# Where weight and activation tiles start in SBUF, and when the first row scales are made: a change to a split-precision decoder trunk

## The chip, the cores and the metric

The kernel runs on one core of a Trainium2 chip. The metric is the device time of one execution, in microseconds (us); three runs before the change took 1011.95, 1014.01 and 1015.58 us, median 1014.01. The engines are TensorE (PE, its weight loads shown apart as PEld), VectorE (DVE), ScalarE (ACT), GpSimd (POOL) and SyncE (SP). [...]

## The reference

A decoder trunk of two layers over 256 tokens of width 1024, all in float32. A layer is a feed-forward block, a token mixer, and a second feed-forward block; the mixer of layer 0 is native sparse attention (nsa), that of layer 1 sliding-window attention (swa). A last norm follows.

```python
def rmsnorm(x, g):
    y = x * rsqrt(mean(x * x, axis=-1, keepdims=True) + 1e-6)
    return y * g

def swiglu(x, w_gu, w_down):             # w_gu: 1024 x 5632, w_down: 2816 x 1024
    g, u = split(x @ w_gu, 2, axis=-1)
    return (silu(g) * u) @ w_down

for i in range(2):
    x = x + 0.5 * swiglu(rmsnorm(x, ffn1_norm[i]), ffn1_w_gu[i], ffn1_w_down[i])
    x = x + mixer[i](rmsnorm(x, mix_norm[i]))
    x = x + 0.5 * swiglu(rmsnorm(x, ffn2_norm[i]), ffn2_w_gu[i], ffn2_w_down[i])
return rmsnorm(x, final_norm)
```

The program calls the four feed-forward blocks ffn0 (layer 0), ffn1 (layer 0, after the nsa mixer), ffn2 and ffn3 (layer 1, around the swa mixer).

## The kernel before, in words

**Split products.** Every float32 product is made of passes in the fp32r type. Weights are fetched as they are (`raw`, five buffers, SP's queue, line 166) and split by `Weights.split` into a high part (a cast to fp32r: tile `whi`, line 150 or 152) and a low part (raw minus high: tile `wlo`, line 178). Each of these tiles is 128 partitions by 1024 + 64 elements, and `place` says at which byte of it the part starts. Activations are transposed on PE (line 199) and split in the same way when they leave PSUM: `xh`, high and low side by side, scaled by the norm's weights out of `prm` (lines 207 and 210).

**Up and gate product** (`gu`, `product` in `ffn`). The columns of `w_gu` are taken in 22 blocks; block f gives 128 columns of the gate (bank 0) and 128 of the up half (bank 1). For each of 8 slices k of the depth and each bank there is a pair of matmuls: the high weights stay in the array while `xh` streams through, high and low together (512 columns, `gu_h`); then the low weights meet the high half of `xh` (256 columns, `gu_l`). So a block is 16 pairs, an ffn 352 pairs or 704 matmuls. Names: `gu_2_0_328` is block 2, bank 0; the last number only tells tiles apart. In ffn0 to ffn3 the high weights start at byte `PLACE_GU` = 64, 128, 192 and 32 of their tile; the low weights and `xh` start at 0. (All tiles begin at a multiple of 256 bytes.)

**Other products** (`RowsProduct`): here the activations stay in the array and the weights stream: 512 columns at a time in the down products (`dn`) and output projections, 256 in the input projections of the mixers (`nin`, `sin`) and in the last two of the three column blocks of ffn3's down product (`LASTW`). For 256 columns both weight parts start at byte 64 (`PLACE_NARROW`), for 512 at 0; the activations start at 0.

**Gate arithmetic.** After a block's last matmul ACT copies the second half of a bank out (`g`, `u`, line 150) and DVE adds the first half (lines 426 and 428). POOL multiplies both by the row scales `rb` (line 155, `ga` and `u`); ACT takes the tanh (`th`, line 430); DVE forms the gate and the product (lines 432 and 155); the result is split into `hh` and `hl` for the down product. `g`, `u`, `ga` and `th` have two buffers each, and even blocks use one pair of PSUM banks, odd blocks another, so block 4 needs the banks of block 2 emptied, and block 2's `u` needs block 0's buffer back.

**Row scales.** A norm's 1/rms per token comes from squares (DVE line 226 and ACT line 230 at the start of ffn0), `n_v` (lines 232, 234), a power on POOL (`n_y`, line 241) and a Newton step on DVE (`n_w`, `n_r`, lines 242 to 245). Two PE transposes (line 406) spread `n_r` over the partitions, and DVE copies the result to `rb` (line 407).

**Order.** The start of ffn0 (`Norm.first`) is written out by hand: its instructions go to the engines as they stand. Elsewhere a scheduler orders them by priorities; all engines then run their queues in that order. In `Norm.first` the loads of x, the identity `ident` (line 294) and the norm weights `prm` (line 296) are spread over the queues of SP and ACT.

Of the kernel before, what the change touches and what calls it, by code (L numbers as in the profile page):

```python
# [21 lines left out]
P = 128  # L22
# [23 lines left out]
PLACE_GU = (64, 128, 192, 32)  # L46
PLACE_NARROW = 64
# [41 lines left out]
def trunk_kernel(tc, x_in, wgu, wdn, nsa_in, nsa_w1, nsa_out, swa_in, swa_out, small, fgain, consts, out):  # L89
# [3 lines left out]
    with ExitStack() as es:  # L93
# [63 lines left out]
        class Weights:  # L157
# [6 lines left out]
            def fetch(self, o, w):  # L164
                raw = wp.tile([P, PIECE], F32, tag="raw", bufs=BUFS["raw"], name=f"{self.name}_r{o}")
                self.last = nc.sync.dma_start(raw[:, :w], self.src[:, o:o + w]).ins
                return raw
# [23 lines left out]


        def transposed(kp, norm, th, tl, tb, engine=None):

            ps = s_bank(f"xt{norm}_{kp}")
            for kk in range(2):
                for t in range(NT):
                    c = ((2 * kp + kk) % 4) * P
                    nc.tensor.transpose(ps[:, kk * S + t * P:kk * S + (t + 1) * P], x[t][kp // 2][:, c:c + P], ident)  # L199
            both = ap_.tile([P, 2, 2, S], F32R, tag="ahl", bufs=BUFS["ahl"], name=f"xh{norm}_{kp}")  # L200
            hi, lo = both[:, :, 0, :], both[:, :, 1, :]

            def evict(kk):
                k = 2 * kp + kk
                g = prm[:, D_GAIN + norm * KD + k:D_GAIN + norm * KD + k + 1]
                if (engine or pick("xh")) == "A":
                    nc.scalar.activation(hi[:, kk, :], ps[:, kk * S:(kk + 1) * S], AF.Copy, scale=g)  # L207
                else:
                    nc.vector.tensor_scalar(hi[:, kk, :], ps[:, kk * S:(kk + 1) * S], g, None, ALU.mult)
                nc.vector.scalar_tensor_tensor(lo[:, kk, :], ps[:, kk * S:(kk + 1) * S], g, hi[:, kk, :],  # L210
                                               ALU.mult, ALU.subtract)
# [7 lines left out]
        def squares(j, c0, c1, v, dve=False):  # L219

            ss = sp.tile([P, NT], F32, tag="ss", bufs=3, name="ss")
            for t in range(NT):
                xc = columns(t, c0, c1)
                if dve and t:
                    junk = ap_.tile([P, 512], F32, tag="junk2", bufs=1, name="junk2")
                    nc.vector.tensor_tensor_reduce(out=junk[:, :c1 - c0], in0=xc, in1=xc, scale=1.0, scalar=0.0,
                                                   op0=ALU.mult, op1=ALU.add, accum_out=ss[:, t:t + 1])
                else:
                    junk = ap_.tile([P, 512], F32, tag="junk", bufs=1, name="junk")
                    nc.scalar.activation(junk[:, :c1 - c0], xc, AF.Square, accum_out=ss[:, t:t + 1])  # L230
            if j == 0:
                nc.vector.tensor_scalar(v, ss, 1.0 / D, EPS, ALU.mult, ALU.add)
            else:
                nc.vector.scalar_tensor_tensor(v, ss, 1.0 / D, v, ALU.mult, ALU.add)

        def row_scale(v, name):
# [6 lines left out]
            nc.vector.tensor_mul(w, w, v)  # L243
            nc.vector.tensor_scalar(w, w, -0.5, 1.5, ALU.mult, ALU.add)
            nc.vector.tensor_mul(r, w, y)
            return r

        class Norm:
# [6 lines left out]
            def block(self, j):  # L255
# [7 lines left out]
                squares(j, c0, c0 + self.widths[j], self.v)  # L263
# [3 lines left out]
            def first(self, wts, product):  # L267


                def load_x(h, queues):  # L270
                    for t, queue in enumerate(queues):
                        queue.dma_start(x[t][h], x_in[t * P:(t + 1) * P, h * 512:(h + 1) * 512])
# [11 lines left out]
                zeros = ap_.tile([P, 512], BF16, tag="junk2", bufs=1, name="zeros")  # L284
# [11 lines left out]
                nc.scalar.dma_start(prm[:, :D_SINK], small[:, :D_SINK])  # L296
# [8 lines left out]
                product(0)  # L305
                wts.split(256, raw[1], 768, "AV")
                leave(1, 3)
                product(2)
                turn(2, 3)
                product(1, 3)  # L310
# [4 lines left out]
                product(4, 6, 5, 7)  # L315
                wts.load(CHUNK, CHUNK, engines="VG")
                for h in range(2):
                    squares(h, h * 512, h * 512 + 512, self.v, True)
                self.r = row_scale(self.v, "n0")


        class RowsProduct:
            def __init__(self, wts, nk, hi, lo, widths, name, tags=("acc",)):
                self.wts, self.nk, self.hi, self.lo = wts, nk, hi, lo
# [38 lines left out]
        def rows_product(wts, nk, hi, lo, done, name):  # L363
            rows = RowsProduct(wts, nk, hi, lo, done.widths, name, ("acc", "out"))
# [18 lines left out]
        def ffn(i, norm, nxt, residual=Residual):  # L383
            with tc.tile_pool(name=f"ffn{i}", bufs=1) as fp:
                wts = Weights(wgu[i], f"gu{i}", (PLACE_GU[i], 0))
# [12 lines left out]

                if i == 0:
                    acc = banks(0)  # L400
                    with tc.manual_schedule():
                        norm.first(wts, lambda *ks: product(0, acc, ks))
                rb = fp.tile([P, S], F32, name="rb")
                ps = t_bank(f"rb{i}")
                for t in range(NT):
                    nc.tensor.transpose(ps[:, t * P:(t + 1) * P], norm.r[:, t:t + 1].to_broadcast([P, P]), ident)
                nc.vector.tensor_copy(rb, ps[:, :S])
                hh, hl = [], []
                for f in range(NF):
                    if i or f:  # L410
                        if i or f > 1:
                            wts.load(f * CHUNK, CHUNK)
                        acc = banks(f)
                        product(f, acc, range(KD))
                    if i == 0 and f == 3:
                        with tc.issue_after(wts.last):
                            nc.sync.dma_start(cst[:, P:], consts[:, P:])
                            nc.sync.dma_start(prm[:, D_SINK:], small[:, D_SINK:])
                    g0 = fp.tile([P, S], F32, tag="g0", bufs=BUFS["g0"], name=f"g0{f}")
                    u0 = fp.tile([P, S], F32, tag="u0", bufs=BUFS["u0"], name=f"u0{f}")  # L420
# [4 lines left out]
                    copy("g0", g0, acc[0][:, S:])  # L425
                    nc.vector.tensor_tensor(g0, acc[0][:, :S], g0, ALU.add)  # L426
                    copy("u1", u0, acc[1][:, S:])
                    nc.vector.tensor_tensor(u0, acc[1][:, :S], u0, ALU.add)  # L428
# [9 lines left out]
                rows_product(Weights(wdn[i], f"dn{i}"), NF, hh, hl, residual(0.25, nxt), f"dn{i}")  # L438
# [120 lines left out]
        def out_tiles(name):  # L559
            both = [ap_.tile([P, 2, 2, S], F32R, tag="ahl", bufs=BUFS["ahl"], name=f"{name}_oh{g}") for g in range(NG)]  # L560
# [456 lines left out]
```

## Time and profile before

| | before |
|---|---|
| runs | 1011.95, 1014.01, 1015.58 us, median 1014.01 |
| profiled execution | 1014.02 us, of which the span of its instructions is 1011.9 us |
| busy time of PE, DVE, ACT, POOL | 977.4 (97%), 694.8 (69%), 555.8 (55%), 499.8 us (49%) |
| granted TensorE clock, mean | 0.991 |
| HBM read | 167.02 MB, 166 GB/s over the span |

A row of a timeline gives the start, the duration of one instruction (or of a run of them, with their count), the engine, the line, the operation with output and input, their shapes, and in brackets the idle time of the engine before it and what ended that. A row of windows gives from:to, the window's length, the busy time and count of each engine asked for, the granted clock (1.00 is full), the share of time in which the DMA engines were busy, and GB/s. A DMA row gives the transfer, the queue it was issued from, its count, its size and the median time from issue to landing.

### The profile page before, as it was taken

What the parts mean: (1) busy time and instruction counts of PE and PEld (TensorE: products, weight loads), DVE (VectorE), ACT (ScalarE), POOL (GpSimd) and SP (SyncE); (2) the same over time, 40 slices, a digit from 0 to 9 for tenths busy, and PEclk for the clock granted to TensorE, in tenths of its full rate; (3) what the DMA queues carried; (4) which work ended last, traced back from release to release, by engine and by line L of the source; (5) the groups of instructions that cost most, each with busy time, mean ns of one, the idle gap of its engine ahead of it and who ended that gap; (6) DMA issues with size and microseconds to landing.
All of it is one profiled execution on the core that took longest, in us unless ns stands there. A gap on an engine that the chain in (4) does not pass through costs nothing. (4 is left out here: it accounts for less than half of the span.)

```text
span 1011.9 us, 15910 instructions
## 1 busy us (share of the span) xinstructions
PE 977.4 (97%) x5626; PEld 845.2 (84%) x5626; DVE 694.8 (69%) x1299; ACT 555.8 (55%) x1041; POOL 499.8 (49%) x490
## 2 busy tenths in 40 slices
PE   7999999998899999999999999999998899999997
PEld 5888888887887788888888888888897688888897
DVE  5877754367798887778445777854279987777533
ACT  5555554456668755555444565554458755555442
POOL 2666673566354126455631566674662016554643
PEclk9999999999899999999999999999999999999999
DMA  7666656552422256666566566656652266666661
GB/s 253 207 192 189 204 173 205 172 167 84 126 84 80 67 152 198 175 202 178 183 186 205 168 205 193 191 176 213 187 150 81 71 200 188 188 187 188 187 188 42
DMA packets 47743, 169.10 MB, mean 167 GB/s; under 512 B 5424, under 2 KB 5808, under 8 KB 47664
## 3 DMA queue, kind: packets, MB, share of 16 engines
q1 hardware_dynamic: 46656, 166.43, 54.7%
q10 hardware_dynamic: 1008, 1.66, 0.4%
q8 instruction: 44, 0.72, 0.3%
q14 instruction: 35, 0.29, 0.1%
HBM read 167.02 MB, written 1.05 MB: 166 GB/s over the span
## 5 line engine op out<-in xcount | busy, mean ns | idle before, releaser
L116 PE MATMUL gu<-xh,gu_h 128*128 128x512 f32 x1408 | 490.0, 394 | 2.6 <-ACT xh L207 2.6
L116 PE MATMUL gu<-xh,gu_l 128*128 128x256 f32 x1408 | 392.3, 280 | 0.0
L116 PEld LDWEIGHTS gu<-xh,gu_h 128*128 128x128 f32 x1408 | 264.9, 189 | 61.0 <-ACT gu_h L150 3.0
L116 PEld LDWEIGHTS gu<-xh,gu_l 128*128 128x128 f32 x1408 | 265.9, 189 | 1.4 <-DVE gu_l L178 0.2
L178 DVE TENSOR_TENSOR gu_l<-gu_r,gu_h 128x1024 fp32r<-128x1024 f32 (+1 forms) x175 | 231.2, 1321 | 30.9 <-ACT gu_h L150 30.0
L150 ACT CAST gu_h<-gu_r 128x1024 fp32r<-128x1024 f32 (+1 forms) x177 | 183.7, 1040 | 42.3 <-PE gu L116 27.2
L150 ACT CAST dn_h<-dn_r 128x1024 fp32r<-128x1024 f32 (+1 forms) x89 | 92.3, 1042 | 103.4 <-PE dn L116 99.8
L116 PE MATMUL dn<-dn_h,hh 128*128 128x512 f32 (+1 forms) x396 | 144.7, 365 | 0.0
L116 PE MATMUL dn<-dn_l,hh 128*128 128x512 f32 (+1 forms) x396 | 144.7, 365 | 0.0
L116 PE MATMUL dn<-dn_h,hl 128*128 128x512 f32 (+1 forms) x396 | 144.5, 365 | 0.0
L178 DVE TENSOR_TENSOR dn_l<-dn_r,dn_h 128x1024 fp32r<-128x1024 f32 (+1 forms) x56 | 73.0, 1308 | 95.9 <-ACT dn_h L150 95.9
L178 POOL TENSOR_TENSOR dn_l<-dn_r,dn_h 128x512 fp32r<-128x512 f32 x66 | 88.7, 1365 | 99.0 <-ACT dn_h L150 98.4
L155 POOL TENSOR_TENSOR ga<-g,rb 128x256 f32<-128x256 f32 x88 | 104.0, 1182 | 62.8 <-DVE g L426 58.4
L155 POOL TENSOR_TENSOR hl<-u,hh 128x256 fp32r<-128x256 f32 x66 | 80.8, 1224 | 51.0 <-ACT hh L150 26.4
L155 POOL TENSOR_TENSOR u<-u,rb 128x256 f32<-128x256 f32 x88 | 68.6, 780 | 59.4 <-DVE u L428 57.5
L430 ACT ACTIVATE th<-ga 128x256 f32<-128x256 f32 x88 | 36.8, 419 | 100.6 <-POOL ga L155 99.5
L116 PEld LDWEIGHTS dn<-dn_h,hh 128*128 128x128 f32 x396 | 74.3, 188 | 12.0
L116 PEld LDWEIGHTS dn<-dn_h,hl 128*128 128x128 f32 x396 | 74.4, 188 | 11.8
L116 PEld LDWEIGHTS dn<-dn_l,hh 128*128 128x128 f32 x396 | 74.3, 188 | 11.8
L150 ACT COPY g<-gu 128x256 f32<-128x256 f32 x88 | 32.8, 373 | 83.4 <-PE gu L116 83.2
L432 DVE SCALAR_TENSOR_TENSOR ga<-th,ga 128x256 f32<-128x256 f32 x88 | 43.4, 493 | 37.9 <-ACT th L430 37.9
L116 PE MATMUL nin<-nin_h,xh 128*128 128x256 f32 (+1 forms) x320 | 62.8, 289 | 2.0 <-DVE r_b L459 1.7
(244 smaller groups left out, 1407.2 us busy)
## 6 DMA issues: line engine op xcount, KB each, us to landing
gu_r<-in_wgu_dram SPq DMA_DIRECT2D x174, 512.0 KB, 4.3
dn_r<-in_wdn_dram SPq DMA_DIRECT2D x87, 512.0 KB, 3.8
nin_r<-in_nsa_in_dram SPq DMA_DIRECT2D x18, 512.0 KB, 3.5
sin_r<-in_swa_in_dram SPq DMA_DIRECT2D x10, 512.0 KB, 3.5
nout_r<-in_nsa_out_dram SPq DMA_DIRECT2D x8, 512.0 KB, 3.6
sout_r<-in_swa_out_dram SPq DMA_DIRECT2D x8, 512.0 KB, 3.7
cmp_r<-in_nsa_w_dram SPq DMA_DIRECT2D x4, 512.0 KB, 4.0
nin_r<-in_nsa_in_dram SPq DMA_DIRECT2D x2, 456.0 KB, 4.0
```

Source lines behind the costliest of these rows:

```text
L116: nc.tensor.matmul(o, w, m, start=start, stop=stop)
L150: nc.scalar.copy(o, i)
L155: (nc.vector if pick(key) == "V" else nc.gpsimd).tensor_tensor(o, a, b, op)
L178: eng.tensor_tensor(lo[:, q:e], raw[:, q:e], hi[:, q:e], ALU.subtract)
L430: nc.scalar.activation(th, ga, AF.Tanh, scale=0.5)
L432: nc.vector.scalar_tensor_tensor(ga, th, 1.0, ga, ALU.add, ALU.mult)
```

## The change

1. The high parts of all four up-and-gate products start at byte 192.
2. In the narrow products the weights start at byte 0 and the activations at 64: `PLACE_NORM` for the two mixers' norms, and in ffn3 a fill of 64 bytes ahead of its tiles (`PLACE_H`), which shifts `hh` and `hl`. ffn3's one 512-wide block has its weights at 64 too. Tiles of activations get 64 elements more (`split_tile`).
3. At the start, `ident` goes to SP's queue, `prm` is second on ACT's queue, and the first 256 columns of weights come third on ACT's queue; their high part is cast on POOL instead of ACT. The squares of x's left half are taken on DVE ahead of the first evictions, those of the right half, both on DVE, after the low part of block 1.
4. The transposes of the row scales stand in block 2 of ffn0, behind its first eight matmuls, and the gate arithmetic of blocks 0 and 1 behind block 2's matmuls. The Newton step is three DVE instructions in place of four, in every norm.

The diff, cut:

```diff
-PLACE_GU = (64, 128, 192, 32)
-PLACE_NARROW = 64
+PLACE_GU = 192
+PLACE_NORM = (0, 64, 0, 0, 64, 0)
+PLACE_H = (0, 0, 0, 64)
...
+        def split_tile(name, place=0):
+            t = ap_.tile([P, 4 * S + 64], F32R, tag="ahl", bufs=BUFS["ahl"], name=name)
+            return t[:, place // 4:place // 4 + 4 * S].rearrange("p (k a t) -> p k a t", k=2, a=2)
...
-            both = ap_.tile([P, 2, 2, S], F32R, tag="ahl", bufs=BUFS["ahl"], name=f"xh{norm}_{kp}")
+            both = split_tile(f"xh{norm}_{kp}", PLACE_NORM[norm])
...
             nc.vector.tensor_mul(w, y, y)
-            nc.vector.tensor_mul(w, w, v)
-            nc.vector.tensor_scalar(w, w, -0.5, 1.5, ALU.mult, ALU.add)
-            nc.vector.tensor_mul(r, w, y)
+            nc.vector.scalar_tensor_tensor(w, w, -0.5, v, ALU.mult, ALU.mult)
+            nc.vector.scalar_tensor_tensor(r, w, 1.5, y, ALU.add, ALU.mult)
...
-                load_x(0, (nc.sync, nc.scalar))
-                nc.scalar.dma_start(ident, consts[:, C_ID:C_ID + P])
-                raw = [wts.fetch(o, n) for o, n in ((0, 256), (256, 768))]
+                load_x(0, 0, nc.sync)
+                load_x(1, 0, nc.scalar)
+                nc.sync.dma_start(ident, consts[:, C_ID:C_ID + P])
                 nc.scalar.dma_start(prm[:, :D_SINK], small[:, :D_SINK])
-                load_x(1, (nc.sync, nc.scalar))
+                raw = [wts.fetch(0, 256, nc.scalar), wts.fetch(256, 768)]
+                load_x(1, 1, nc.scalar)
+                load_x(0, 1, nc.sync)
...
+                left = squares(0, 512, "V")
                 turn(0, 1)
...
-                wts.split(0, raw[0], 256, "AG")
+                wts.split(0, raw[0], 256, "GG")
...
                 wts.load(CHUNK, CHUNK, engines="VG")
-                for h in range(2):
-                    squares(h, h * 512, h * 512 + 512, self.v, True)
+                right = squares(512, 1024, "V")
+                mean(0, self.v, left)
+                mean(1, self.v, right)
                 self.r = row_scale(self.v, "n0")
+                product(1, *range(KD))
...
-                self.wts.place = (0, 0) if w == 512 else (PLACE_NARROW, PLACE_NARROW)
+                self.wts.place = (self.place * (w == 512),) * 2
...
+                if PLACE_H[i]:
+                    fill(fp, "place", PLACE_H[i])
+                wts = Weights(wgu[i], f"gu{i}", (PLACE_GU, 0))
...
+                        if f == len(early):
+                            product(f, acc, ks[:len(early)])
+                            broadcast_scale()
+                            ks = ks[len(early):]
+                        product(f, acc, ks)
...
+                    if f == len(early):
+                        for args in left:
+                            gated(*args)
...
+                    if f < len(early):
+                        left.append((f, g0, u0))
+                    else:
+                        gated(f, g0, u0)
```

(`early` holds blocks 0 and 1 in ffn0 and is empty in the other three, where the broadcast stays ahead of block 0.)

What this does to the order at three places. On ACT, the DMAs at the program's start, before the change:

```order
L272 DMA x_73<-in_x_dram 128x512
L294 DMA ident<-in_consts_dram 128x128
L296 DMA prm<-in_small_dram 128x48
L272 DMA x_74<-in_x_dram 128x512
L299 ACT_TABLE_LOAD
L299 ACTIVATE warm<-mhalf 128x2
L207 ACTIVATE xh_0_123<-xt_0_118,prm 128x256
```

The same rows of ACT's queue after the change (`gu_r_109` are the 256 columns):

```order
L280 DMA x_73<-in_x_dram 128x512
L304 DMA prm<-in_small_dram 128x48
L168 DMA gu_r_109<-in_wgu_dram 128x256
L280 DMA x_74<-in_x_dram 128x512
L309 ACT_TABLE_LOAD
L309 ACTIVATE warm<-mhalf 128x2
L214 ACTIVATE xh_0_130<-xt_0_125,prm 128x256
```

`prm` moves ahead to second, `ident` leaves for SP's queue (second there, in the place of the 256 columns), and those 256 columns of weights come third here.

On PE, around the transposes of the row scales, before the change (the last two pairs of block 1 and the first pair of block 2):

```order
L116 MATMUL gu_1_0_265<-xh_3_168,gu_h_217 128x512
L116 MATMUL gu_1_0_265<-xh_3_168,gu_l_218 128x256
L406 MATMUL rb_244<-ident,n_r 128x128 x2
L116 MATMUL gu_1_1_266<-xh_3_168,gu_h_217 128x512
L116 MATMUL gu_1_1_266<-xh_3_168,gu_l_218 128x256
L116 MATMUL gu_2_0_328<-xh_0_123,gu_h_318 128x512
L116 MATMUL gu_2_0_328<-xh_0_123,gu_l_319 128x256
```

On PE around the same transposes after the change (block 2, slices 1 and 2 of the depth):

```order
L118 MATMUL gu_2_1_302<-xh_0_130,gu_h_291 128x512
L118 MATMUL gu_2_1_302<-xh_0_130,gu_l_292 128x256
L424 MATMUL rb_311<-ident,n_r 128x128 x2
L118 MATMUL gu_2_0_301<-xh_1_136,gu_h_291 128x512
L118 MATMUL gu_2_0_301<-xh_1_136,gu_l_292 128x256
L118 MATMUL gu_2_1_302<-xh_1_136,gu_h_291 128x512
L118 MATMUL gu_2_1_302<-xh_1_136,gu_l_292 128x256
```

The transposes move from ahead of block 1's last pair to behind block 2's fourth pair, ten matmuls later.

On DVE, from the first Newton step to the copy of `rb` and what follows it, before the change:

```order
L242 TENSOR_TENSOR n_w<-n_y 128x2
L243 TENSOR_TENSOR n_w<-n_w,n_v 128x2
L178 TENSOR_TENSOR gu_l_319<-gu_r_316,gu_h_318 128x1024
L244 TENSOR_SCALAR n_w<-n_w 128x2
L178 TENSOR_TENSOR gu_l_325<-gu_r_322,gu_h_324 128x1024
L245 TENSOR_TENSOR n_r<-n_w,n_y 128x2
L178 TENSOR_TENSOR gu_l_382<-gu_r_379,gu_h_381 128x1024
L407 COPY rb<-rb_244 128x256
L426 TENSOR_TENSOR g_299<-gu_1_0_265,g_299 128x256
L178 TENSOR_TENSOR gu_l_388<-gu_r_385,gu_h_387 128x1024
L432 SCALAR_TENSOR_TENSOR ga_250<-th_251,ga_250 128x256
```

The same stretch of DVE's queue after the change:

```order
L252 TENSOR_TENSOR n_w<-n_y 128x2
L180 TENSOR_TENSOR gu_l_292<-gu_r_289,gu_h_291 128x1024
L253 SCALAR_TENSOR_TENSOR n_w<-n_w,n_v 128x2
L180 TENSOR_TENSOR gu_l_298<-gu_r_295,gu_h_297 128x1024
L254 SCALAR_TENSOR_TENSOR n_r<-n_w,n_y 128x2
L180 TENSOR_TENSOR gu_l_381<-gu_r_378,gu_h_380 128x1024
L468 TENSOR_TENSOR g_283<-gu_1_0_90,g_283 128x256
L180 TENSOR_TENSOR gu_l_387<-gu_r_384,gu_h_386 128x1024
L470 TENSOR_TENSOR u_284<-gu_1_1_91,u_284 128x256
L425 COPY rb<-rb_311 128x256
L180 TENSOR_TENSOR gu_l_446<-gu_r_443,gu_h_445 128x1024
L439 SCALAR_TENSOR_TENSOR ga_339<-th_340,ga_339 128x256
```

The copy of `rb` had one low part between it and `n_r`; now it has two, and the additions of block 1 (`g_283`, `u_284`), with one more low part right behind it, ahead of the first gate (`ga`, line 432 before, 439 after). The addition into `u_362`, which empties block 2's second bank, follows behind a further low part.

More of the change, by code (lines that the diff above doesn't have):

```diff
@@ L217, in columns, with squares @@
             return x[t][c0 // 512][:, c0 % 512:c0 % 512 + c1 - c0]
-        def squares(j, c0, c1, v, dve=False):
+        def squares(c0, c1, engine="A"):
             ss = sp.tile([P, NT], F32, tag="ss", bufs=3, name="ss")
@@ L223, in squares @@
                 xc = columns(t, c0, c1)
-                if dve and t:
-                    junk = ap_.tile([P, 512], F32, tag="junk2", bufs=1, name="junk2")
+                junk = ap_.tile([P, 512], F32, tag="junk", bufs=1, name="junk")
+                if engine == "V":
                     nc.vector.tensor_tensor_reduce(out=junk[:, :c1 - c0], in0=xc, in1=xc, scale=1.0, scalar=0.0,
@@ L228, in squares, with mean @@
                 else:
-                    junk = ap_.tile([P, 512], F32, tag="junk", bufs=1, name="junk")
                     nc.scalar.activation(junk[:, :c1 - c0], xc, AF.Square, accum_out=ss[:, t:t + 1])
+            return ss
+        def mean(j, v, ss):
             if j == 0:
@@ L262, in block @@
                         evict(1)
-                squares(j, c0, c0 + self.widths[j], self.v)
+                mean(j, self.v, squares(c0, c0 + self.widths[j]))
                 if j == len(self.widths) - 1:
@@ L267, in first, with load_x @@
             def first(self, wts, product):
-                def load_x(h, queues):
-                    for t, queue in enumerate(queues):
-                        queue.dma_start(x[t][h], x_in[t * P:(t + 1) * P, h * 512:(h + 1) * 512])
+                def load_x(t, h, queue):
+                    queue.dma_start(x[t][h], x_in[t * P:(t + 1) * P, h * 512:(h + 1) * 512])
                 evict = {}
@@ L282, in leave @@
                         evict[k // 2](k % 2)
-                zeros = ap_.tile([P, 512], BF16, tag="junk2", bufs=1, name="zeros")
+                zeros = ap_.tile([P, 512], BF16, name="zeros")
                 nc.vector.memset(zeros, 0.0)
@@ L361, in block, with rows_product @@
                 return acc
-        def rows_product(wts, nk, hi, lo, done, name):
-            rows = RowsProduct(wts, nk, hi, lo, done.widths, name, ("acc", "out"))
+        def rows_product(wts, nk, hi, lo, done, name, place=0):
+            rows = RowsProduct(wts, nk, hi, lo, done.widths, name, ("acc", "out"), place)
             for j in range(len(done.widths)):
@@ L397, in product, with broadcast_scale, gated @@
                             do(*args)
+                early = []
                 if i == 0:
-                    acc = banks(0)
+                    early = [banks(f) for f in range(2)]
                     with tc.manual_schedule():
-                        norm.first(wts, lambda *ks: product(0, acc, ks))
+                        norm.first(wts, lambda f, *ks: product(f, early[f], ks))
                 rb = fp.tile([P, S], F32, name="rb")
[L404 to L407, printed above, removed]
-                hh, hl = [], []
[L409 to L420, printed above, removed]
+                def broadcast_scale():
+                    ps = t_bank(f"rb{i}")
+                    for t in range(NT):
+                        nc.tensor.transpose(ps[:, t * P:(t + 1) * P], norm.r[:, t:t + 1].to_broadcast([P, P]), ident)
+                    nc.vector.tensor_copy(rb, ps[:, :S])
+                hh, hl = [], []
+                left = []
+                def gated(f, g0, u0):
                     ga = fp.tile([P, S], F32, tag="ga", bufs=BUFS["ga"], name=f"ga{f}")
@@ L559, in out_tiles @@
         def out_tiles(name):
-            both = [ap_.tile([P, 2, 2, S], F32R, tag="ahl", bufs=BUFS["ahl"], name=f"{name}_oh{g}") for g in range(NG)]
+            both = [split_tile(f"{name}_oh{g}") for g in range(NG)]
             return [b[:, :, 0, :] for b in both], [b[:, :, 1, :] for b in both]
```

40 lines of the change are left out of this document (26 added, 14 removed).

## The prediction

> **What bounds the kernel now.** First the page's busy shares and slices, to see which engine the span belongs to.
>
> ```profile
> span 1011.9 us, 15910 instructions
> ...
> PE 977.4 (97%) x5626; PEld 845.2 (84%) x5626; DVE 694.8 (69%) x1299; ACT 555.8 (55%) x1041; POOL 499.8 (49%) x490
> ...
> PE   7999999998899999999999999999998899999997
> ...
> PEclk9999999999899999999999999999999999999999
> ```
>
> TensorE (PE) is busy 97% of the span, at full clock but for a start. An edit pays if PE's matmuls follow each other faster or if PE waits less; work of the other engines counts where PE ends up waiting for it. So the second view is the windows, 80 us out of the middle of each ffn's up-and-gate stage, in program order (high parts at 64, 128, 192 and 32 bytes). The columns after the window are its length and then busy time (with count) of PE, PEld, DVE, ACT and POOL, then the granted clock, the DMA share and GB/s.
>
> ```profile
> 40.00:120.00 80.00, 80.00 (x472) 70.92 (x471) 62.28 (x97) 45.17 (x78) 50.49 (x48) 1.00 0.66 192
> 385.00:465.00 80.00, 80.00 (x457) 69.85 (x456) 61.92 (x94) 45.16 (x76) 44.27 (x47) 1.00 0.64 191
> 575.00:655.00 80.00, 80.00 (x472) 70.74 (x471) 62.26 (x97) 44.77 (x77) 50.53 (x49) 1.00 0.66 195
> 845.00:925.00 80.00, 80.00 (x457) 69.77 (x457) 60.42 (x95) 44.97 (x75) 46.79 (x48) 1.00 0.65 191
> ```
>
> PE never idles in any of them and the clock is 1.00, yet ffn1 and ffn3 (128 and 32 bytes) get 457 matmuls through where ffn0 and ffn2 (64 and 192) get 472. A pair of matmuls (512 columns, then 256) takes 80/236 = 0.339 us in the one and 80/228.5 = 0.350 in the other. Those two stages are what a change of place can win. The third view is the same windows cut to the whole stages of ffn1, ffn2 and ffn3, counting the instructions of the tile `gu` alone (PE, PEld, DVE, ACT).
>
> ```profile
> 364.40:489.60 125.20, 124.67 (x704) 107.95 (x703) 17.53 (x42) 15.86 (x43) 1.00 0.63 185
> 550.40:671.50 121.10, 120.56 (x704) 105.65 (x703) 17.52 (x42) 15.65 (x42) 1.00 0.64 188
> 818.70:943.60 124.90, 124.37 (x704) 107.55 (x703) 17.52 (x42) 15.91 (x43) 1.00 0.63 186
> ```
>
> The same 704 matmuls take 124.67 and 124.37 us at 128 and 32 bytes, 120.56 at 192.
>
> **The sum, part by part.** It is made against the profiled execution, 1014.02 us (span 1011.9 and 2.1 around it), which is also the median of the runs (1014.01). 0.3% of it, 3.0 us, is about what a measurement of this kernel can tell from no change.
>
> *High parts at 192.* The arithmetic of the stages is unchanged; ffn1 and ffn3 get ffn2's place and, I take it, its pace: (124.67 − 120.56) + (124.37 − 120.56) = 7.9 us less, all on PE and so on the path. ffn0 goes from 64 to 192, and both places show 472: 0. Bounds: −7.9, and for no effect at all 0.
>
> *Narrow products.* Input projections and the last half of ffn3's down product stream 256 columns of weights, at 64 bytes, against activations at 0. Afterwards the weights lie at 0 and the activations at 64. Two pieces of the nsa input projection, and the end of ffn3:
>
> ```profile
> 284.08 0.40 PE L116 MATMUL nin<-nin_h,xh 128*128 128x256 f32 x2
> ...
> 288.32 0.40 PE L116 MATMUL nin<-nin_h,xh 128*128 128x256 f32 x2
> ```
> ```profile
> 302.01 0.39 PE L116 MATMUL nin<-nin_h,xh 128*128 128x256 f32 x2
> ...
> 305.41 0.39 PE L116 MATMUL nin<-nin_h,xh 128*128 128x256 f32 x2
> ```
> ```profile
> 980.00:1000.00 20.00, 20.00 (x172) 1.00 0.21 66
> ```
>
> 36 matmuls lie between the first two rows, 0.118 us each; 30 between the next two, 0.113 each: the same form at the same addresses runs at two paces. ffn3's end (about 170 starts in 20 us) keeps the slow one, 0.118. On the path stand 2 × 132 such matmuls in ffn3's down product and 240 in the swa input projection. Best end: all get the fast pace, 504 × 0.0047 = −2.4. Other end: the new offset costs what the bad places cost a pair, (0.350 − 0.339)/2 per matmul, 504 × 0.0055 = +2.8. The nearest row is ffn0's window: there too the stationary tile (the weights) starts 64 bytes past the moving one, and the pace is the fast one. Its stream is 512 columns wide, not 256, so I take half of the best end: −1.2. The nsa projection gets 0, since part of it is fast already.
>
> *The start.*
>
> ```profile
> ident<-in_consts_dram ACTq DMA_DIRECT2D x1, 64.0 KB, 4.0
> prm<-in_small_dram ACTq DMA_DIRECT2D x1, 24.0 KB, 7.2
> ```
> ```profile
> 1.66 0.45 ACTq L296 DMA_DIRECT2D prm<-in_small_dram  x1
> ...
> 8.93 0.47 ACT L207 ACTIVATE xh<-xt,prm 128x256 fp32r<-128x256 f32 x1 [4.81 <-DMA prm<-in_small_dram]
> 9.31 0.39 ACT L150 CAST gu_h<-gu_r 128x256 fp32r<-128x256 f32 x1
> 9.44 0.48 DVE L210 SCALAR_TENSOR_TENSOR xh<-xt,prm,xh 128x256 fp32r<-128x256 f32 x1 [8.31 <-ACT xh L207]
> ...
> 10.07 1.19 PE L116 MATMUL gu<-xh,gu_h 128*128 128x512 f32 x2 [2.56 <-ACT xh L207]
> ```
>
> The first matmul waits for an eviction, and that for the norm weights `prm`, third on ACT's DMA queue, which land 7.2 us after their issue. As second they are issued 0.48 us earlier (an issue takes 0.45). The first weights' 128 KB take their old slot as third, and if they land as late as `prm` did (8.9), the cast, now on POOL, and the first matmul come at about 9.5. `ident` on SP's queue replaces that 128 KB piece as second, so SP's later transfers issue no later. The two squares put ahead of DVE's evictions are covered by its 8.31 us of idling; ACT loses two squares and a cast. PE runs these first matmuls at half clock (windows of 3.4 us: busy time, clock):
>
> ```profile
> 9.80:13.20 3.40, 3.13 (x11) 0.50 0.24 54
> ```
>
> If full clock comes no earlier than about 13.2, starting 0.5 us earlier is worth half. I take −0.3 (0 to −0.5).
>
> *Blocks 1 to 4 of ffn0.* First, what the row scales cost now: two more of these windows, then the timelines of PE, DVE, POOL and ACT.
>
> ```profile
> 23.40:26.80 3.40, 0.99 (x7) 1.00 0.59 171
> 26.80:30.20 3.40, 3.40 (x12) 0.51 0.93 314
> ```
> ```profile
> 25.99 0.43 PE L406 MATMUL rb<-ident,n_r 128*128 128x128 f32 x2 [2.41 <-DVE n_r L245]
> ...
> 27.05 0.63 PE L116 MATMUL gu<-xh,gu_h 128*128 128x512 f32 x1
> ...
> 30.25 0.40 PE L116 MATMUL gu<-xh,gu_h 128*128 128x512 f32 x1
> ```
> ```profile
> 18.34 1.80 DVE L226 CUSTOM_DVE_ANT_0 junk<-x 128x512 f32<-128x512 f32 x1
> ...
> 21.25 0.68 DVE L226 CUSTOM_DVE_ANT_0 junk<-x 128x512 f32<-128x512 f32 x1
> ...
> 23.43 1.23 DVE L178 TENSOR_TENSOR gu_l<-gu_r,gu_h 128x1024 fp32r<-128x1024 f32 x1
> ...
> 25.78 0.15 DVE L245 TENSOR_TENSOR n_r<-n_w,n_y 128x2 f32<-128x2 f32 x1
> ...
> 26.98 0.42 DVE L407 COPY rb<-rb 128x256 f32<-128x256 f32 x1
> ...
> 36.58 0.41 DVE L428 TENSOR_TENSOR u<-gu,u 128x256 f32<-128x256 f32 x1
> ```
> ```profile
> 18.18 3.12 POOL L178 TENSOR_TENSOR gu_l<-gu_r,gu_h 128x512 fp32r<-128x512 f32 x2 [4.57 <-PE gu L116]
> ```
> ```profile
> 38.96 0.37 ACT L150 COPY g<-gu 128x256 f32<-128x256 f32 x1 [0.32 <-PE gu L116]
> ```
>
> PE waits 2.41 us for `n_r`, and the idle window is followed by one at half clock: five pairs at 0.64 instead of 0.34, 1.5 us. Together 3.9. Afterwards PE runs into block 2, whose first low part (the 23.43 row) ends at about 24.6; PE, which stopped at 23.58 with a pair of block 1 left, would want it at about 24.1 or, after the earlier start, 23.8: 0.5 to 0.8 us of waiting. Eight matmuls later (1.4 us) `n_r`, behind one more low part, is just there: 0.1 to 0.2. Too little idling for the clock. The fused row scales save a 0.16 us DVE instruction in each norm: hidden behind the low parts, 0. Gain so far 3.0.
>
> But the copy of `rb` now stands behind two low parts (1.23 each) and two additions (0.41) that were partly behind it: it ends about 2 us later on the old clock, near 29.3 for 27.4. Behind it wait POOL's multiplications of blocks 0 and 1, the tanh, DVE's two products, POOL's subtraction that frees block 0's `u` buffer, ACT's copy into that buffer, and DVE's addition, which empties block 2's second bank for block 4. In the trace the addition (36.58 row) ended 9.6 us after `rb`; block 3's first bank was done at 38.9 (last row), so there were 2 us in hand. Now it ends at 38.2 to 38.9 while PE, 3.0 earlier, wants the bank at about 36.4: a new wait of some 2.1 us. That wait is this part's dearest guess: the order shows what queues, not how long it takes. Taken: −3.0 + 2.1 = −0.9, from −3.1 (no new wait) to +1.5 (a longer one, with a window at half clock after it).
>
> [...]
>
> Sum: 1014.0 − 7.9 − 1.2 − 0.3 − 0.9 = **1003.7 us**.
>
> **Rivals.**
>
> *No new wait at block 4.* If POOL's and DVE's work behind `rb` packs better than before (ACT has less to do at the start), the 2.1 us do not appear: 1001.6. For it: 9.6 us for a chain of eight steps hold much queueing that may close up. Against: the four low parts that block 2 and 3 need are issued ahead. 25%.
>
> *The new offset is no better for narrow streams.* 0 to +2.8 in place of −1.2: 1004.9 to 1007.7. For it: the pace changes at fixed addresses, so something besides the address sets it. 20%.
>
> *Place does not matter.* ffn1 and ffn3 would be slower for another reason in their surroundings, and 7.9 + 1.2 us stay: 1012.8, within 0.3%. Against: the four windows have the same load on all engines (DMA 0.64 to 0.66, clock 1.00). 6%. [...]
>
> *Slower: the fast pace is a state that a stage falls into, not its address.* The nsa projection shows two paces at one address. If at 192, with the new start, all four stages settle in the 0.350 pace, ffn0 and ffn2 lose what ffn1 and ffn3 keep: 2 × 352 × 0.011 = +7.9, with the start and blocks −1.2: 1020.7 (narrow at 0). It decides from a mean pair of 0.349 on: 1408 × (0.349 − 0.3445) = 6.3 over the mean of now is more than 3.0 + 1.2. Against: ffn2 holds its pace at 192 for 120 us through 0.5 us of stalls (121.10 − 120.56). 4%.
>
> **How the numbers follow.** Forecast 45%, no new wait 25%, narrow no better 20%, place without effect 6%, all slow 4%. The first three are faster by over 0.3% (below 1011.0): 0.90; same 0.06; slower 0.04. The range: the low end is the rival without a new wait, 1001.6, less half a narrow gain and some of the scatter of the runs (1011.95 to 1015.58): 1000.0. The high end is narrow at its worst, 1007.7, with a little for a longer wait at block 4: 1008.5. Left out is about 15%.
>
> **What would show it.** The windows of ffn1 and ffn3 should count 472 in 80 us, their stages last 121; ffn3's end should count about 177 in 20 us for the full narrow gain. PE's wait at `rb` should be below 0.3 us and no half-clock window follow it; a wait of about 2 us should stand at block 4's second bank, with `u` as its releaser; the first `gu` matmul should start near 9.5. The forecast is wrong if a stage at 192 counts 457, or if PE's lost time between 23 and 45 us exceeds 4 us.

## The result: 1001.93 us, ratio 0.989

Four runs of the changed kernel took 1000.10, 1001.73, 1002.14 and 1006.02 us, median 1001.93; the kernel before took 1011.57 to 1015.58, median 1012.98. The ratio is 0.9894 (95% interval 0.9856 to 0.9931): 10.7 us less, between 7 and 14.6. Forecast were 1003.7 us and a range of 1000.0 to 1008.5.

The page of the changed kernel, its lines for the span and the busy shares:

```profile
span 999.9 us, 15905 instructions
...
PE 966.6 (97%) x5626; PEld 836.7 (84%) x5626; DVE 688.5 (69%) x1297; ACT 551.4 (55%) x1036; POOL 511.1 (51%) x491
```

PE is as full as before over a span 12.0 us shorter. The windows out of the middle of the four gate-and-up stages, in program order (columns as in the prediction):

```profile
40.00:120.00 80.00, 80.00 (x459) 70.13 (x458) 62.47 (x97) 44.48 (x78) 51.66 (x49) 1.00 0.67 198
385.00:465.00 80.00, 80.00 (x472) 71.00 (x472) 61.84 (x97) 45.23 (x77) 54.11 (x50) 1.00 0.66 198
575.00:655.00 80.00, 80.00 (x472) 70.76 (x471) 63.02 (x96) 46.04 (x79) 52.44 (x50) 1.00 0.67 198
835.00:915.00 80.00, 80.00 (x472) 70.76 (x471) 62.62 (x98) 44.41 (x76) 53.00 (x49) 1.00 0.66 195
```

ffn1 and ffn3 went from 457 matmuls to 472. But ffn0, which had 472 at byte 64, has 459 at 192: nearly what the bad places had. The whole stages of ffn1, ffn2 and ffn3, instructions of `gu` alone:

```profile
360.80:482.00 121.20, 120.63 (x704) 106.03 (x703) 17.52 (x42) 15.66 (x42) 1.00 0.63 187
542.60:663.80 121.20, 120.62 (x704) 105.72 (x704) 17.52 (x42) 15.65 (x42) 1.00 0.63 188
810.40:931.70 121.30, 120.65 (x704) 105.71 (x704) 17.50 (x42) 16.02 (x43) 1.00 0.65 191
```

124.67 and 124.37 us of PE became 120.63 and 120.65. The start and the row scales, as DMA rows and PE rows of ffn0:

```profile
gu_r<-in_wgu_dram ACTq DMA_DIRECT2D x1, 128.0 KB, 6.5
...
prm<-in_small_dram ACTq DMA_DIRECT2D x1, 24.0 KB, 3.8
```
```profile
8.66 0.74 PE L118 MATMUL gu<-xh,gu_h 128*128 128x512 f32 x2 [1.61 <-POOL gu_h L154]
...
22.25 0.38 PE L118 MATMUL gu<-xh,gu_l 128*128 128x256 f32 x1 [0.28 <-DVE gu_l L180]
...
23.53 0.43 PE L424 MATMUL rb<-ident,n_r 128*128 128x128 f32 x2
...
35.44 0.49 PE L118 MATMUL gu<-xh,gu_h 128*128 128x512 f32 x1 [1.32 <-DVE u L470]
```

`prm` lands 3.8 us after its issue instead of 7.2, and the first matmul, at 8.66 for 10.07, now waits for the cast of the first weights (POOL, `gu_h`), which are third on ACT's queue. The transposes at 23.53 wait for nothing. The new stop at block 4 is there, 1.32 us, with `u` as its releaser. Behind that stand, on ACT and then on DVE:

```profile
34.55 0.37 ACT L152 COPY u<-gu 128x256 f32<-128x256 f32 x1 [0.27 <-POOL hl L157]
```
```profile
34.96 0.42 DVE L470 TENSOR_TENSOR u<-gu,u 128x256 f32<-128x256 f32 x1 [1.72 <-ACT u L152]
```

POOL's subtraction frees the buffer, ACT copies into it, DVE adds: the chain of the prediction.

Where the 12.0 us of the two profiled spans came from, by first and last matmul of each stage:

| stage | before, us | after, us | difference |
|---|---|---|---|
| first `gu` matmul of ffn0 | 10.07 | 8.66 | −1.4 |
| gate and up, ffn0 | 127.12 | 127.49 | +0.4 |
| nsa input projection, with the mixer's work among it | 119.74 | 117.20 | −2.5 |
| gate and up, ffn1 | 125.31 | 121.16 | −4.2 |
| swa input projection, likewise | 40.54 | 39.95 | −0.6 |
| gate and up, ffn3 | 124.98 | 121.18 | −3.8 |
| down product, ffn3 | 61.19 | 61.19 | 0 |

The 2.5 us of the nsa mixer are in no sum of the prediction. The clock shows them. Windows of 3.4 us there (PE's busy time and count, clock), before:

```profile
242.00:245.40 3.40, 3.40 (x18) 0.52 0.52 154
252.20:255.60 3.40, 3.40 (x16) 0.51 0.38 98
265.80:269.20 3.40, 3.27 (x16) 0.50 0.44 130
```

and after, at the same distances:

```profile
241.30:244.70 3.40, 3.40 (x18) 0.51 0.53 154
251.50:254.90 3.40, 3.40 (x29) 1.00 0.46 143
265.10:268.50 3.40, 3.40 (x32) 1.00 0.53 154
```

Three stretches at half clock became one. That need not be the change's doing: another execution of the changed kernel had two (below).

### The profile page after: what moved, and what is told of

Same layout as the page of the kernel before. It is cut to its first block, busy times and chain, and to the rows that moved or that the text cites. A ratio compares the mean times of both kernels' runs of the same rounds, so it can differ in the third digit from the quotient of the medians.

```text
span 999.9 us, 15905 instructions
## 1 busy us (share of the span) xinstructions
PE 966.6 (97%) x5626; PEld 836.7 (84%) x5626; DVE 688.5 (69%) x1297; ACT 551.4 (55%) x1036; POOL 511.1 (51%) x491
## 5 line engine op out<-in xcount | busy, mean ns | idle before, releaser
L118 PE MATMUL gu<-xh,gu_h 128*128 128x512 f32 x1408 | 483.0, 391 | 2.9 <-POOL gu_h L154 1.6
L180 DVE TENSOR_TENSOR gu_l<-gu_r,gu_h 128x1024 fp32r<-128x1024 f32 (+1 forms) x175 | 228.3, 1304 | 24.3 <-ACT gu_h L152 24.1
L157 POOL TENSOR_TENSOR ga<-g,rb 128x256 f32<-128x256 f32 x88 | 113.3, 1287 | 64.6 <-DVE g L468 58.7
L157 POOL TENSOR_TENSOR hl<-u,hh 128x256 fp32r<-128x256 f32 x66 | 85.1, 1290 | 51.7 <-ACT hh L152 25.5
L157 POOL TENSOR_TENSOR u<-u,rb 128x256 f32<-128x256 f32 x88 | 66.4, 754 | 35.0 <-DVE u L470 33.1
```

Of the source, the lines that this page charges most:

```text
L118: nc.tensor.matmul(o, w, m, start=start, stop=stop)
L157: (nc.vector if pick(key) == "V" else nc.gpsimd).tensor_tensor(o, a, b, op)
L180: eng.tensor_tensor(lo[:, q:e], raw[:, q:e], hi[:, q:e], ALU.subtract)
```

## The experiments

Two theories on ffn0. P (place): 192 is a slow place for ffn0. S (state): places 64 and 192 each allow a fast pace (0.340 us a pair) and a slow one (0.350), and a stop of PE sets which one follows. Paces are the time from the start of one pair to the start of the next.

**Place alone, in the kernel before.**

```diff
-PLACE_GU = (64, 128, 192, 32)
+PLACE_GU = (192, 192, 192, 192)
```

> The kernel before with all four high parts at byte 192 and nothing else changed (its program order is the same, instruction by instruction). Two theories of the pace of a gate-and-up stage. P (place): the pace belongs to the place and the stage, and ffn0 is slow at 192. S (state): 192 has a fast state (0.340 us a pair) and a slow one (0.350), and a stop of PE near the stage's start sets which one it keeps. Both expect ffn1 and ffn3 to drop from 125.3 and 125.0 us to 121.2. P expects 459 matmuls in 40 to 120 us of ffn0 and about 1014.0 - 7.9 + 3.6 = 1009.7. S leaves ffn0 open: 472 and about 1006.1 if its last stop (at the row scales, as before the change) falls well, else the time of P.

1001.2 us, ratio to the kernel before 0.9874 (0.9841 to 0.9908). Windows of ffn0, ffn1 and ffn3 (PE alone):

```profile
40.00:120.00 80.00, 80.00 (x472) 1.00 0.61 196
385.00:465.00 80.00, 80.00 (x473) 1.00 0.62 198
835.00:915.00 80.00, 80.00 (x472) 1.00 0.62 197
```

ffn1 and ffn3 as expected, and ffn0 is fast at 192, against P. But the time is lower than either theory's (1009.7 and 1006.1). In the profile the rest is the nsa mixer (117.48 us, one half-clock stretch) and the start, 8.98 with the old order of the DMAs: the first matmul of the profile before, at 10.07, was itself a late one (`prm` landed in 6.1 us here, 7.2 there).

**Narrow products as before.**

```diff
-PLACE_NORM = (0, 64, 0, 0, 64, 0)
-PLACE_H = (0, 0, 0, 64)
+PLACE_NARROW = 64
+PLACE_NORM = (0, 0, 0, 0, 0, 0)
+PLACE_H = (0, 0, 0, 0)
...
-                self.wts.place = (self.place * (w == 512),) * 2
+                self.wts.place = (0, 0) if w == 512 else (PLACE_NARROW, PLACE_NARROW)
```

> The changed kernel with the narrow products back at weights 64, activations 0. If the new offset is what shortened the nsa input projection (119.7 to 117.2 us) and the swa one (40.5 to 40.0), both come back, and the time is about 1001.7 + 3.1 = 1004.8. If those stages are shorter for another reason (their start falls differently), nothing changes: 1001.7. ffn3's down product showed no gain and should stay at 61.2 us. ffn0 is as in the changed kernel: by P (pace belongs to place and stage) 459 matmuls in 40 to 120 us; by S (a state that a stop sets) 459 or 472, 3.5 us apart.

1002.18 us, 0.9878 (0.985 to 0.9907): no loss that can be told. The nsa projection is back at 119.74 us, but with three half-clock stretches in place of one (below); the swa one at 40.55; ffn3's down product unchanged at 61.20.

**ffn0 at 64 again**, and **the right half's squares on ACT**.

```diff
-PLACE_GU = 192
+PLACE_GU = (64, 192, 192, 192)
...
```

> The changed kernel with ffn0's high parts at byte 64 as before the change, the other three at 192. P (pace belongs to the place): ffn0 is back at 472 matmuls in 40 to 120 us and the time is about 1001.7 - 3.6 = 998.1. S (a stop of PE sets one of two states, at 64 as at 192): the stop of 0.3 us ahead of block 2's first low part is still there, and ffn0 may stay at 0.350 us a pair, 1001.7.

```diff
-                right = squares(512, 1024, "V")
+                right = squares(512, 1024)
```

> The changed kernel with the squares of x's right half on ACT instead of DVE, so that DVE makes block 2's first low part some 2 to 3 us earlier, and PE no longer stops for it or for the row scales. S (a stop sets the state): ffn0 keeps the 0.340 us a pair of its block 1, 472 matmuls in 40 to 120 us, about 1001.7 - 0.6 - 3.5 = 997.6, if the wait of 1.3 us at block 4 does not set it anew. P (ffn0 is slow at 192): 459, and only the stop is saved: 1001.1.

1002.51 us (0.9882, 0.9855 to 0.991) and 1002.59 us (0.9876, 0.9837 to 0.9916). The clearest view is PE in ffn0 ahead of the stop at block 4 and behind it. In order: narrow products undone, ffn0 at 64, squares on ACT.

```profile
24.50:33.50 9.00, 9.00 (x55) 1.00 0.75 267
40.00:120.00 80.00, 80.00 (x459) 1.00 0.62 198
```
```profile
24.50:33.50 9.00, 9.00 (x53) 1.00 0.76 269
45.00:120.00 75.00, 75.00 (x443) 1.00 0.62 197
```
```profile
23.50:32.50 9.00, 9.00 (x53) 1.00 0.70 242
40.00:120.00 80.00, 80.00 (x473) 1.00 0.62 198
```

The first goes from fast to slow (in block 3 a pair takes 0.340 us, from block 5 on 0.350), the other two from slow to fast, each at the stop, and stay there to the end of the stage. The place does not change within a stage. So there are two paces at one place, as S has it, and 64 is no safer than 192: at 64, too, block 3 ran at 0.350. With the squares on ACT the stop for the low part is gone and the one at `u` is 0.8 us; ffn0 took 3.9 us less than in the changed kernel (123.56 from first matmul to last), but the nsa stage took 121.14, with four half-clock stretches, and no time was gained.

**Three buffers for u** (the entry `u0` of `BUFS`, without the rest of its line).

```diff
-"u0": 2
+"u0": 3
```

> The changed kernel with three buffers for u instead of two, so that ACT's copy of block 2's u need not wait for POOL's subtraction in block 0 (PE's order and DVE's are the same). Theory of the wait at block 4 (u's buffer comes back late): the copy comes about 2 us earlier and the wait of 1.3 us goes. [...] By theory S (a stop of PE sets one of two paces for what follows) there is then one stop fewer to set ffn0's pace; 472 or 459 matmuls in 40 to 120 us, whichever block 3 had. Time 1001.9 - 1.4 = 1000.5, and 3.5 less if ffn0 is in the fast pace.

1001.48 us (0.9877, 0.9834 to 0.9919). The stop at block 4 is gone, and one row of PE is new:

```profile
47.80 0.50 PE L118 MATMUL gu<-xh,gu_h 128*128 128x512 f32 x1 [0.95 <-DVE u L470]
```

The buffer was the cause at block 4. The third buffer did not clear the backlog: a stop of 0.95 us came two blocks later. It left the pace at 0.340, so a stop need not swap it.

**Breaks put in by hand.** Two transposes more in blocks 4, 7, 10, 13, 16 and 19 of ffn1 to ffn3 (results unused); in ffn1 of row scales that have long been there, in ffn2 and ffn3 of the last block's g.

```diff
+                        if i and f in (4, 7, 10, 13, 16, 19):
+                            n = (0, 2, 2, 1)[i]
+                            product(f, acc, ks[:n])
+                            ps = t_bank(f"turn{i}_{f}")
+                            for t in range(NT):
+                                src = norm.r[:, t:t + 1].to_broadcast([P, P]) if i == 1 else g0[:, t * P:(t + 1) * P]
+                                nc.tensor.transpose(ps[:, t * P:(t + 1) * P], src, ident)
+                            ks = ks[n:]
```

> The changed kernel with two more transposes on PE in blocks 4, 7, 10, 13, 16 and 19 of ffn1, ffn2 and ffn3 (none of their results is used): in ffn1 of row scales that are long there, so that PE only breaks its rhythm; in ffn2 and ffn3 of the previous block's g, which DVE writes late, so that PE may stop for it. Theory S (a stop of PE sets one of two paces): ffn1 keeps 0.340 us a pair or changes at few of its six breaks, ffn2 and ffn3 change between 0.340 and 0.350 behind several of their twelve; each stage grows by 1 to 2 us for the transposes and up to 3.6 for the pace. Theory P (192 is fast in ffn1 to ffn3, and what slows ffn0 is ffn0's own): all stay at 0.340 behind every break.

1017.22 us in one run. In ffn1, where nothing is waited for, the pace behind the six breaks is 0.350, 0.340, 0.350, 0.340, 0.350, 0.340: each break swaps it, where S as put expected few changes without a stop. In ffn2 it is 0.350, then 0.340 five times; in ffn3 0.340, 0.340, 0.350, 0.350, 0.340, 0.350: five swaps in twelve breaks. PE waited for g at five of the twelve (0.1 to 1.0 us), and one of these five swapped the pace. P would have all at 0.340. The stages took 124.02, 123.49 and 127.22 us.

**How many transposes.** The same blocks, ready row scales only: one transpose in ffn1, four in ffn2, two in ffn3.

```diff
...
+                            for n in range((0, 1, 4, 2)[i]):
+                                t = n % NT
+                                nc.tensor.transpose(ps[:, n * P:(n + 1) * P], norm.r[:, t:t + 1].to_broadcast([P, P]), ident)
...
```

> As the run with extra transposes, but all of row scales that are long there, so that PE never stops, only breaks its rhythm, in blocks 4, 7, 10, 13, 16 and 19: one transpose in ffn1, four in ffn2, two in ffn3. If two transposes swap the pace each time (as in ffn1 of that run), ffn3 goes 0.340, 0.350, 0.340 and so on through its six breaks. If it is their number that decides, one and four differ from two, and four, twice two, may leave the pace alone; if any break swaps it, all three stages alternate.

1008.77 us in one run. Windows of 13 us between the breaks of ffn3, from ahead of the first to behind the last:

```profile
825.50:838.50 13.00, 13.00 (x79) 1.00 0.64 202
841.00:854.00 13.00, 13.00 (x76) 1.00 0.68 222
858.00:871.00 13.00, 13.00 (x78) 1.00 0.63 205
874.00:887.00 13.00, 13.00 (x77) 1.00 0.60 189
891.00:904.00 13.00, 13.00 (x79) 1.00 0.58 186
908.00:921.00 13.00, 13.00 (x76) 1.00 0.60 186
924.50:937.50 13.00, 13.00 (x78) 1.00 0.56 176
```

Two transposes swap the pace six times of six (78 or 79 matmuls, then 76 or 77). One (ffn1) and four (ffn2) leave it alone at all twelve breaks; the window behind the first break of each:

```profile
388.00:401.00 13.00, 13.00 (x79) 1.00 0.65 210
```
```profile
571.00:584.00 13.00, 13.00 (x78) 1.00 0.62 198
```

So a break alone does not swap the pace: two transposes of ready row scales do, one and four do not. Whether the length of the break decides is not shown. In ffn2 of the run before, PE waited for g at one break only; at the other five the starts of the pairs around the transposes lie 0.48 to 0.50 us apart, about as around the row scales' (0.48 to 0.49), and only the first two of the five swapped. Why the pace swaps was not found.

**Other places.** High parts at 0, 64, 160 and 224 bytes in ffn0 to ffn3, and at 128, 0, 32 and 128; other distances for the narrow products.

```diff
-PLACE_GU = 192
-PLACE_NORM = (0, 64, 0, 0, 64, 0)
-PLACE_H = (0, 0, 0, 64)
+PLACE_GU = (0, 64, 160, 224)
+PLACE_NORM = (0, 0, 0, 0, 128, 0)
+PLACE_H = (0, 0, 0, 128)
...
```

> The changed kernel with the high parts at 0, 64, 160 and 224 bytes in ffn0 to ffn3; swa projection's activations and ffn3's h at 128, the nsa projection's at 0 (weights at 0). If a place has a pace of its own: 64 as in ffn0 before, 0.340 or, after an unlucky stop, 0.350; 160 and 224 as 32 before (0.351, not steady), 0 open. If only stops matter, all four at 0.340 or 0.350 steadily. Narrow: if 64 bytes apart is what made 0.118 us, 128 or 0 apart gives 0.113 in ffn3's end; if it is a state there too, either.

```diff
+PLACE_GU = (128, 0, 32, 128)
+PLACE_NORM = (0, 192, 0, 0, 32, 0)
+PLACE_H = (0, 0, 0, 192)
...
```

> As before this, with the high parts at 128, 0, 32 and 128 bytes in ffn0 to ffn3, the nsa projection's activations at 192, the swa projection's at 32, ffn3's h at 192. If place sets the pace, 128 is at 0.351 in ffn0 and ffn3 as it was in ffn1, and 32 at 0.351 in ffn2 as it was in ffn3; 0 agrees with the run that has 0 in ffn0. If the stage set it, ffn2 stays at 0.340 at 32.

1014.42 and 1015.17 us, one run each. The four stages in order, then ffn3's narrow products; first kernel, then second:

```profile
45.00:125.00 80.00, 80.00 (x455) 1.00 0.61 194
385.00:465.00 80.00, 80.00 (x459) 1.00 0.61 192
575.00:655.00 80.00, 80.00 (x460) 1.00 0.59 190
845.00:925.00 80.00, 80.00 (x466) 1.00 0.61 191
985.00:1005.00 20.00, 20.00 (x169) 1.00 0.06 18
```
```profile
45.00:125.00 80.00, 80.00 (x456) 1.00 0.62 196
385.00:465.00 80.00, 80.00 (x464) 1.00 0.61 196
575.00:655.00 80.00, 80.00 (x458) 1.00 0.59 187
845.00:925.00 80.00, 80.00 (x457) 1.00 0.59 189
985.00:1005.00 20.00, 20.00 (x172) 1.00 0.08 28
```

128 gives 456 and 457 in two other stages, 32 gives 458 in a third: these paces belong to the place. 0 gives 455 and 464, 160 gives 460, 224 gives 466; whether these have a second pace, single runs can't tell. Only 64 and 192 reach 472, and 64 in ffn1 stood at 459 from its start on. The end of ffn3 in the changed kernel, for comparison:

```profile
971.00:991.00 20.00, 20.00 (x172) 1.00 0.11 41
```

For ffn3's 256 columns the change's distance of 64 bytes is thus no faster than the old places (172 in 20 us in the prediction's row); 192 (second kernel) gives 172 as well, and 128 (first) is slower.

**The changed kernel again, the old places, and no stops**, on one chip with more runs each.

> The changed kernel itself, on the same chip as the two kernels beside it. Theory: 8 us of its gain are the places of ffn1 and ffn3 and are in every run; the rest comes and goes by about 3.5 us with ffn0's pace and by 1.2 to 2.4 us with the half-clock windows in the nsa mixer. So stages ffn1 and ffn3 of 121.2 us again, ffn0 at 459 or 472 matmuls in 40 to 120 us, and one to three half-clock windows in the nsa mixer (one before). Rival: ffn0's pace and the mixer's windows are the change's own and repeat: 459 and one.

1001.46 us, 0.9894 (0.9871 to 0.9918). This time ffn0 is fast:

```profile
40.00:120.00 80.00, 80.00 (x473) 1.00 0.63 198
```

The same program had 459 in the first profile, with nearly the same two stops (0.28 and 1.32 us there, 0.25 and 1.33 here). In both, blocks 2 and 3 run at 0.350; behind the stop at block 4 the first profile stays there and this one goes to 0.340. The nsa mixer had two half-clock stretches for one. So the change fixes neither ffn0's final pace nor the mixer's clock.

```diff
-PLACE_GU = 192
+PLACE_GU = (64, 128, 192, 32)
...
```

> The changed kernel with the high parts back at 64, 128, 192 and 32 bytes: the start, the row scales and the narrow products alone. Stages ffn1 and ffn3 at 125.3 and 125.0 us. If the rest of the change is worth the 0.3 + 0.9 + 1.2 us of the prediction, it is 2.4 us faster than the kernel before; if place is all that counts on average, it is as fast as the kernel before within 1 us. From the profiles alone (start 1.4, row scales about 2): up to 3.5 us faster with ffn0 in the fast pace.

1011.50 us, 0.9973 (0.9958 to 0.9988): the start, the row scales and the narrow products are worth 0.27%, 2.7 us (1.2 to 4.3). The places are the rest, 0.9973 − 0.9894 = 0.0079, 8.0 us (roughly 5 to 11, by the two intervals).

```diff
-"u0": 2
+"u0": 3
...
-                right = squares(512, 1024, "V")
+                right = squares(512, 1024)
```

> The changed kernel with the right half's squares on ACT and three buffers for u. If these are the two causes of PE's stops in ffn0, no stop of over 0.2 us is left between 15 and 60 us; rival: POOL has too much to do between blocks 2 and 6, and a stop of some 0.9 us stays at block 6. Time: the stops of 0.3 and 1.3 us and their restarts are worth about 2 us, 999.9; half-clock windows in the nsa mixer, whose end stood at about 313.7 or 317.3 us in all runs wherever ffn0 ended, may swallow it: then no difference from the changed kernel beside it.

1002.22 us, 0.9876 (0.9857 to 0.9896), against 0.9894 (0.9871 to 0.9918) of the changed kernel beside it: the same within the intervals. The stops are gone. Block 1 runs at 0.350; from the transposes of block 2 on the pace is 0.340, until this, in block 10:

```profile
65.44 0.28 PE L118 MATMUL gu<-xh,gu_l 128*128 128x256 f32 x1
65.60 0.50 PE L118 MATMUL gu<-xh,gu_h 128*128 128x512 f32 x1
```

The second row starts 0.16 us after the first instead of 0.11; the two pairs there take 0.389 and 0.453 us, and from then on a pair takes 0.350. The nsa stage ended at 310.6 us here, so its ends are not held to 313.7 or 317.3, as that expectation had it.

**ffn0, read across the profiles.** The change itself put two transposes of row scales into block 2. In the kernel with the squares on ACT PE waits for nothing in that block ahead of them, and yet:

```profile
22.49 0.39 PE L118 MATMUL gu<-xh,gu_h 128*128 128x512 f32 x1
...
22.83 0.38 PE L424 MATMUL rb<-ident,n_r 128*128 128x128 f32 x2
...
23.75 0.40 PE L118 MATMUL gu<-xh,gu_h 128*128 128x512 f32 x1
...
24.10 0.40 PE L118 MATMUL gu<-xh,gu_h 128*128 128x512 f32 x1
```

Up to the transposes a pair takes 0.340 us (the first of them starts where the next pair would), behind them 0.350. In the kernel without stops they swapped it the other way, 0.350 to 0.340. In the ten profiles with the change's order and ffn0 at 64 or 192, block 3 has the other pace than block 1 in nine; where a stop at block 4 remained, it swapped the pace again in six of eight. Block 1 itself had 0.340 in six of the ten and 0.350 in four.

**The nsa mixer, read across the twelve profiles with the old or the new narrow places.** Its stage's length goes above all by the number of half-clock stretches in it:

| half-clock stretches | stage, us (old narrow places marked *) |
|---|---|
| 1 | 117.20, 117.48*, 117.09 |
| 2 | 118.30, 118.59, 118.89, 118.89 |
| 3 | 119.74*, 119.74*, 119.43 |
| 4 | 121.14, 120.96 |

About 1.2 us for each. The stretches are 3.4 us long and come and go between executions of one kernel (the changed one had 1 and 2). At one number the old narrow places are some 0.3 us longer (117.48 against 117.20 and 117.09, 119.74 against 119.43), a difference as small as the scatter at two stretches; the two kernels with other distances, 0 and 192 bytes, took 119.57 and 119.19 with two.

## Why the prediction was right, and where it was not

*The places* were the right main term: 7.9 us forecast, 124.67 + 124.37 − 120.63 − 120.65 = 7.8 in the stages, 8.0 (roughly 5 to 11) between the two kernels that differ in nothing else. It had the right reason too: 472 against 457 at equal load, and 128 and 32 were slow again in other stages.

*"ffn0 goes from 64 to 192, and both places show 472: 0"* is the step that failed. Both places also have 0.350, and in the first profile ffn0 had it from block 2 to the end: 312 pairs × 0.010 = 3.1 us lost. The rival that pace is a state was right in its mechanism and wrong in its size: it took all four stages into the slow state, 1020.7 us (its 2 × 352 × 0.011 is 7.7, not 7.9). What was held against it was a misreading: the 0.5 us in ffn2 were no stalls. With all 716 matmuls of that window counted, PE is busy for 121.10 of its 121.10 us; the 0.5 us were 12 matmuls of other tiles. So ffn2's pace had not been put to the test. ffn1 to ffn3 at 192 were fast in all kernels that left their order alone, ffn0 in some. What sets ffn0 apart in the rows is that its rhythm is broken in the middle of the stage: by the two transposes that the change put into block 2, and by stops.

*Narrow products*, −1.2: mis-sized. ffn3's end gained 0 (172 in 20 us before and after). The swa stage took 40.54 to 40.55 us with the old places in three profiles and 39.95 to 40.43 with the new ones in nine: −0.1 to −0.6. The nsa stage goes by the clock, with perhaps −0.3 from the places. So −0.1 to −0.9, and too little to show in the time of the kernel with the old narrow places. Half of a best end that no row showed for this form was too much, and the row that I leaned on, ffn0's fast pace at 64, was a state.

*The start*, −0.3: 1.4 against this profile of before, since both `prm` and the weights landed sooner than I allowed; but the old order gave 8.98 in another run, and the changed kernels 7.82 to 9.36. I took one execution's 10.07 for the kernel's own.

*Blocks 1 to 4*, −0.9: the mechanism holds, stop for stop. The wait at `rb` went (2.41 us before), and with it the half-clock window (23.40:26.80 and 26.80:30.20 are both at 1.00 after the change, so 0.28 us of idling at 22.25 brought none, as the prediction had it); the wait for the low part was 0.28 us (forecast 0.5 to 0.8), the new one at block 4 1.32, by the chain named (forecast 2.1). With ffn0 in the fast pace behind block 4 the stage took 124.74 us for 127.12, so −2.4 with what the start's half-clock window gave (9.80:13.20 at 0.50 before, none there in that profile). DVE's squares of 128x512 were slow beside POOL's low parts in both profiles, 1.80 us before, 1.78 and 1.66 after (at 16.13 and 17.95), against 0.68 and 0.69 without them.

*The parts against the whole.* The start, the row scales and the narrow products were forecast at 2.4 us together and measured at 2.7 (1.2 to 4.3). Place alone came out at 0.9874 where its 8 us would give 0.992, which its interval (to 0.9908) just leaves out; 9.3 to 10.8 us would fit both. Place alone was thus as fast as the whole change, and that the other parts add to it is seen only at the old places. In its profile the nsa mixer and the start were both lucky; whether that held in its other runs can't be seen, and it stays open.

*Luck.* The sum came within 1.8 us of the median in part because misses cancelled. In the first profile ffn0 lost 3.1 us by its pace and the narrow products gave less than forecast, while the start gave 1.1 us more and the nsa mixer 2.5 us that no term held.

## What to carry to other kernels

Where a stage's matmul count per window differs at equal load and clock, as 457 and 472 did here, look at the start addresses of stationary and moving tiles, and compare the steady middle of stages, not their totals. Before a pace is put down to a place, run the same program twice (459 and 473 in ffn0 here) and put short breaks of different lengths into the stage: a pace that swaps there, as at two transposes, is a state, though one that does not, as at one and four, may be one too. And a saving ahead of a stretch like the nsa mixer (PE busy for 50.74 of the 60 us from 220 to 280 in the profile of before) should be judged over many runs: the one to four half-clock windows in it moved its length by up to some 4 us (117.09 to 121.14).

## What the hardware showed that was not expected

- The pace of a fixed stream of matmuls has two steady values at one pair of addresses, 0.340 and 0.350 us a pair, kept for over 100 us. A hiccup that cost two pairs 0.16 us in all (0.389 + 0.453 for 0.680) swapped it, as did two 128x128 transposes of ready row scales, in twelve of twelve breaks put in by hand; one or four did not, in six breaks each. Breaks much like these, with two transposes of g, swapped it in some cases only, and stops of 1.32 and 1.33 us in two executions of one program ended differently.
- Places differ as well: 128 and 32 bytes gave 456 to 458 matmuls in 80 us in every stage tried. PE was busy for 80.00 of 80.00 us in the windows of 457 and of 472, so no wait on another engine shows there; yet in the kernel before with its places alone changed, ffn1 went from 457 (128 bytes) to 473 (192).
- Runs of one kernel scatter by 6 to 7 us (the kernel before on one chip: 1010.62 to 1016.92). Two causes are seen in the profiles: ffn0's pace, about 3 us, and half-clock stretches of 3.4 us in the nsa mixer, 1.2 us each. In the profile of before, the five stretches ahead of the end start 17.1, 215.0, 10.2 and 13.7 us apart: 5, 63, 3 and 4 times 3.413 us, the recorded length of each.
